# Reciprocal roots of all norms: one power on GpSimd in place of eleven VectorE steps

## The chip, the core and the metric

The kernel runs on one core of a Trainium2 chip. The metric is the time of one execution on the device, in microseconds (us); lower is better. The engines are named as in the profile: PE (TensorE, matrix products and transposes), DVE (VectorE), ACT (ScalarE), POOL (GpSimd) and SP (SyncE, which here issues nearly all DMAs). Each engine works through its own queue strictly in order; an instruction that waits for another engine or for a DMA holds up all that stands behind it on the same engine.

## What is computed

One layer of a hybrid decoder for one sequence of 2048 tokens with 1024 channels, in float32. The root that the change is about stands in `rmsnorm`, which is used for the two layer inputs, for the outputs of the attention and of the state-space model (SSM), and for the final output:

```python
def rmsnorm(x, g):
    y = x32 * lax.rsqrt(jnp.mean(x32 * x32, axis=-1, keepdims=True) + EPS)
    return y * g

h = rmsnorm(x, g_mix) * (1.0 + sc_m) + sh_m          # sc, sh, gt come from silu(c) @ w_ada + b_ada
q, k, v, f_logit, u = jnp.split(h @ w_in, ...)
attn = rmsnorm(forgetting_attention(q, k, v, log_sigmoid(f_logit + b_fgate)), g_attn_out)   # 8 heads of 64
ssm = rmsnorm(s5_ssm(u, ...), g_ssm_out)                                                    # 32 groups of 16
x = x + gt_m * (jnp.concatenate([attn, ssm], axis=-1) @ w_out)
h = rmsnorm(x, g_ffn) * (1.0 + sc_f) + sh_f
gate_pre, val = jnp.split(h @ w_up, 2, axis=-1)                                             # D_FF = 2816
x = x + gt_f * ((silu(causal_dwconv(gate_pre)) * val) @ w_down)
return rmsnorm(x, g_final)
```

## The kernel before

**Work and tiles.** Activations lie with channels on the 128 partitions and tokens along the free axis, in four blocks b = 0 to 3 of 512 tokens. Products are made at nearly full float32 accuracy from a high and a low part of both operands (`hi` and `lo`, three matmuls for each product). So the weights are cast on ACT (`w_hi`, L86 and L121) and their rest is taken on DVE (`w_lo`, L87).

**Order of the stages.** First the inputs of blocks 2, 3, 1 and 0 are normed and projected, with the SSM's tables made beside that; then the SSM; then attention, block by block, mixed with the projections. For each block `mix_t(b)` loads attention and SSM outputs, norms both and transposes the SSM's rows (L1221); `out_proj(b)` multiplies by `w_out` (L1247); `h2_of` norms the result for the feed-forward. Blocks 0 and 1 have their up and down projections (L1273, L1305 to L1307) while attention of blocks 1 to 3 fills the gaps of the other engines. After `out_proj(2)` and `out_proj(3)`, attention is closed; blocks 2 and 3 then go through `up_pair` (L1397) and `down_both` (L1545 to L1547, with L1627) together. At the very end `finish_last` norms and writes block 3 in two halves of 256 tokens (p = 0 and 1).

**A norm's factor.** The squares of all channels are summed into `sq_acc` (L353, L356 and L357), four matmuls with ones (`token_sums`, L365) give the sum of each token as 128x4 numbers in PSUM, `rsqrt_mean` (L182 to L197) makes 1/sqrt(sum/width + eps) of them, four transposes (`over_channels`, L371) spread that over the channels, and ACT copies it to `rt` (L391, or L1713 at the end). There are 21 such roots: 4 for the inputs, 4 each for the SSM and the attention outputs, 4 for the feed-forward inputs, 5 for the outputs (the last block has two).

**The old root.** L185 on DVE makes v = sum/width + eps (`rs_v`). L187 and L188 shift and subtract its bits for a first guess (`rs_i`); three rounds of L193, L194 and L195 refine it (`rs_t`, `rs_y`). All of it works on 128x4 numbers, twice on 128x2.

**The end of attention.** The names for a head pair: L1012, L1013 and L1015 are the scores, ACT L1022 and L1023 the exponentials and their high part, DVE L1024 the low part, DVE L1032 and L1029 the sums, PE L1033 and L1037 the products with the values. When a pair is done: sums to PE (L1061), reciprocal on DVE (L1063), ACT L1065, transposes L1068, scaling on DVE (L1069), a DMA that writes it (L1070). `mix_t` then reads attention (L1208) and SSM rows (L1209), ACT squares the SSM rows (L1211), and after the root DVE scales them (L1217), PE transposes (L1221), ACT applies the gain (L1223) and splits (L400, with DVE L401). `mix_t(3)` puts its rows into the pool `late`.

**What sets the order.** The kernel is written as a tile program; a planner simulates the whole of it with its own costs and writes one fixed order for each engine. `tc.high_priority()` puts a part ahead of others that are ready at the same moment, `tc.issue_after(...)` keeps a part back until an instruction has been placed. So another root can move instructions that have nothing to do with it. `pad` only takes memory, so that the tiles behind it keep their addresses.

Of the kernel before, what the change touches and what calls it, by code (L numbers as in the profile page):

```python
# [12 lines left out]
F32 = mybir.dt.float32  # L13
F32R = mybir.dt.float32r
BF16 = mybir.dt.bfloat16
I32 = mybir.dt.int32
AF = mybir.ActivationFunctionType
ALU = mybir.AluOpType
# [4 lines left out]
P = 128  # L23
# [10 lines left out]
EPS = 1e-6  # L34
NEG = -1e30
WSLOT = 1024
RSQRT_MAGIC = float(0x5F3759DF)
MAGIC = 12582912.0
FFG = (6, 6, 5, 5)
XB = 6  # L40
# [85 lines left out]
def hybrid_layer(ctx, tc, x, c_t, w_ada, b_col, gains, w_flat, bf_row, a_re, a_im, log_dt,  # L126
                 sb_re, sb_im, sc_re, sc_im, dskip, glu, bglu, conv, out):
    nc = tc.nc
    V, A, G, T, Q = nc.vector, nc.scalar, nc.gpsimd, nc.tensor, nc.sync

    const = ctx.enter_context(tc.tile_pool(name="const", bufs=1))
    wpool = ctx.enter_context(tc.tile_pool(name="w", bufs=2))
    small = ctx.enter_context(tc.tile_pool(name="small", bufs=4))
# [3 lines left out]
    def pad(pool, n):  # L137
        if n:
            pool.tile([P, n // 4], F32, name="pad", tag="pad", bufs=1)

    pad(const, 32)
    pad(small, 0)

    @contextmanager
    def behind(ins=None):
# [8 lines left out]
    make_identity(nc, ident)  # L154
    identb = const.tile([P, P], BF16, name="identb")
    V.tensor_copy(identb, ident)
    ones = const.tile([P, 1], F32, name="ones")
    G.memset(ones, 1.0)
    sel = const.tile([P, 2], F32, name="sel")
# [22 lines left out]
    def rsqrt_mean(ss, n, width):  # L182

        v = small.tile([P, 8], F32, name="rs_v")[:, :n]
        V.tensor_scalar(out=v, in0=ss, scalar1=1.0 / width, scalar2=EPS, op0=ALU.mult, op1=ALU.add)  # L185
        i = small.tile([P, 8], I32, name="rs_i", bufs=2)[:, :n]
        V.tensor_scalar(out=i, in0=v.bitcast(I32), scalar1=1, scalar2=None, op0=ALU.logical_shift_right)  # L187
        V.tensor_scalar(out=i, in0=i, scalar1=-1.0, scalar2=RSQRT_MAGIC, op0=ALU.mult, op1=ALU.add)  # L188
        y = i.bitcast(F32)
        for _ in range(3):  # L190
            t = small.tile([P, 8], F32, name="rs_t", bufs=2)[:, :n]
            r = small.tile([P, 8], F32, name="rs_y")[:, :n]
            V.tensor_tensor(out=t, in0=y, in1=y, op=ALU.mult)  # L193
            V.scalar_tensor_tensor(out=t, in0=t, scalar=-0.5, in1=v, op0=ALU.mult, op1=ALU.mult)  # L194
            V.scalar_tensor_tensor(out=r, in0=t, scalar=1.5, in1=y, op0=ALU.add, op1=ALU.mult)  # L195
            y = r
        return y  # L197


    sil = const.tile([P, 8], F32, name="sil")  # L200
# [172 lines left out]
    def norm_sums(acc, ps_fn):  # L373
        ps = ps_fn()
        token_sums(ps, acc, 0, 4)
        return rsqrt_mean(ps[:, 0:4], 4, D)

    def norm_factor(acc, ps_fn, direct=False):

        ps = ps_fn()  # L380
        token_sums(ps, acc, 0, 4)
        r = rsqrt_mean(ps[:, 0:4], 4, D)
        return spread(r, ps_fn, direct)
# [808 lines left out]
    def mix_t(b, tag="row", late_parts=None, ps_fn=None):  # L1192
# [13 lines left out]
        for s in range(4):  # L1206
# [5 lines left out]
            rows.append(t)  # L1212
        res = {}
        rs = rsqrt_mean(ss[:, 0:4], 4, 512)
        for s in range(4):
            f = rows[s][:, 1]
# [570 lines left out]
    for b in range(2):  # L1787
        i = 0
        for g, n in enumerate(FFG):
# [10 lines left out]
            for d in range(8):  # L1800
# [9 lines left out]
                if last and d == OPD:  # L1810
                    with behind():
                        r = norm_sums(sq1 if b == 0 else sqb, op_ps)
# [129 lines left out]
```

## Time and profile before

| | |
|---|---|
| time, median of 3 runs | 2587.67 us (2587.0 to 2597.44) |
| the profiled execution: time, span | 2591.18 us, 2589.5 us |
| PE busy | 2494.1 us, 96% of the span, mean granted clock 0.983 |
| DVE busy | 2048.6 us, 79% |
| ACT busy | 1253.0 us, 48% |
| POOL busy | 151.7 us, 6% |
| moved by DMA | 516.37 MB, mean 199 GB/s |

The profiled execution took 3.5 us more than the median, and its time is 1.7 us more than its span. Busy is the time in which an engine had work, whatever its speed: PE is granted a lower clock at some places, and matmuls there count as busy for longer. In a table of windows a row gives the stretch and its length, then for PE, PEld (weight loads), DVE, ACT and POOL the busy us with the number of instructions, then PE's granted clock (1.00 is full), the share of time that the DMA engines were busy, and GB/s. In a row of a timeline the columns are start, duration, engine, line, operation, what is written and read, shape and count, and in brackets the idle time of this engine before it and what ended that.

### The profile page before, as it was taken

The numbers are of one execution on the slowest core, as the hardware profiler recorded it, in microseconds if no ns is written. First come the engines' busy times: TensorE is split into PE (matmuls) and PEld (weight loads), VectorE is DVE, ScalarE is ACT, GpSimd is POOL, SyncE is SP. The second block draws the span as 40 slices with busy tenths as digits, with TensorE's granted clock in tenths as the row PEclk, the third lists the DMA queues.
The fourth block names the chain that finished last, engine by engine and source line by source line (L and its number), as shares of the span: only waits on it lengthen the run. The fifth ranks groups of instructions, "written<-read, shape, count | busy, mean of one in ns | idle before, by whom it ended". The sixth has DMA issues, their size and how long they took to land.

```text
span 2589.5 us, 35781 instructions
## 1 busy us (share of the span) xinstructions
PE 2494.1 (96%) x12107; PEld 2044.2 (79%) x12107; DVE 2048.6 (79%) x3954; ACT 1253.0 (48%) x2122; POOL 151.7 (6%) x160
## 2 busy tenths in 40 slices
PE   6899999998999999999999999999989999999997
PEld 3788877887788888888878888888768888887876
DVE  7989688976787878877877777776589889886777
ACT  3323255654454545555555655556554555553213
POOL 0001000000000000000000000000002333320000
PEclk8999999999899999999999999999999999999998
DMA  8477987667556655656556555556733443447573
GB/s 313 153 256 223 309 257 210 200 184 244 178 185 219 209 185 184 196 179 211 189 198 226 185 179 186 177 184 219 256 101 130 166 160 134 159 153 286 196 279 119
DMA packets 269608, 516.37 MB, mean 199 GB/s; under 512 B 27985, under 2 KB 114897, under 8 KB 269425
## 3 DMA queue, kind: packets, MB, share of 16 engines
q1 hardware_dynamic: 267600, 508.84, 59.6%
q0 software_dynamic: 1280, 4.20, 0.4%
q8 instruction: 96, 1.57, 0.3%
q10 hardware_dynamic: 544, 1.05, 0.1%
q14 instruction: 88, 0.71, 0.1%
HBM read 374.32 MB, written 139.59 MB: 198 GB/s over the span
## 4 chain that ended last, share of the span: by engine, by line
PE 73%; DMA 10%; DVE 10%; ACT 2%; issue 2%; SPq 2%; POOL 0%; POOLq 0%; ACTq 0%; DVEq 0%
PE ff_ps L1273 18%; PE ff_ps L1247 6%; PE up_x L1397 5%; PE up_z L1397 4%; PE up_y L1397 4%; PE ff_ps L1305 3%; PE ff_ps L1307 3%; PE ff_ps L1306 3%; PE o_ps L1033 2%; PE o_ps L1037 2%; DMA wada<-in_w_ada 2%; PE qs_ps L485 2%; PE acc_x L1627 2%; DMA w_raw<-in_w_flat 2%; PE vq_ps L485 1%
## 5 line engine op out<-in xcount | busy, mean ns | idle before, releaser
L86 ACT CAST w_hi<-w_raw 128x1024 fp32r<-128x1024 f32 (+4 forms) x187 | 173.6, 929 | 273.3 <-DMA w_raw<-in_w_flat 63.4
L1273 PE MATMUL ff_ps<-h_hi,w_hi 128*128 128x512 f32 x704 | 276.7, 394 | 1.0 <-ACT h_hi L403 0.8
L1273 PE MATMUL ff_ps<-h_hi,w_lo 128*128 128x512 f32 x704 | 276.7, 393 | 0.9 <-DMA w_lo<-wlo 0.9
L1273 PE MATMUL ff_ps<-h_lo,w_hi 128*128 128x512 f32 x704 | 276.8, 393 | 0.0
L87 DVE TENSOR_TENSOR w_lo<-w_raw,w_hi 128x1024 fp32r<-128x1024 f32 (+4 forms) x187 | 199.6, 1067 | 54.1 <-ACT w_hi L86 48.9
L1024 DVE TENSOR_TENSOR pl<-pf,ph 128x512 fp32r<-128x512 f32 (+1 forms) x320 | 194.5, 617 | 23.3 <-ACT ph L1023 22.6
L1023 ACT CAST ph<-pf 128x512 fp32r<-128x512 f32 (+1 forms) x320 | 178.0, 568 | 58.6 <-PE o_ps L1033 54.8
L1032 DVE TENSOR_TENSOR acc<-acc,pf 128x512 f32<-128x512 f32 (+2 forms) x264 | 159.2, 604 | 45.1 <-ACT pf L1022 39.5
L1273 PEld LDWEIGHTS ff_ps<-h_hi,w_hi 128*128 128x128 f32 x704 | 132.7, 189 | 29.0 <-ACT h_hi L403 1.5
L1273 PEld LDWEIGHTS ff_ps<-h_hi,w_lo 128*128 128x128 f32 x704 | 132.8, 189 | 28.6 <-DMA w_lo<-wlo 1.3
L1022 ACT ACTIVATE pf<-sc_ps 128x512 f32<-128x512 f32 (+3 forms) x184 | 96.6, 528 | 121.0 <-PE sc_ps L1013 74.7
L1273 PEld LDWEIGHTS ff_ps<-h_lo,w_hi 128*128 128x128 f32 x704 | 132.8, 189 | 27.5 <-issue 0.3
L121 ACT CAST w_hi<-w_raw 128x1024 fp32r<-128x1024 f32 (+2 forms) x100 | 96.7, 967 | 106.2 <-PE ff_ps L1273 50.8
L1306 PE MATMUL ff_ps<-act_lo,w_hi 128*128 128x512 f32 x352 | 138.2, 393 | 0.0
L1307 PE MATMUL ff_ps<-act_hi,w_lo 128*128 128x512 f32 x352 | 138.1, 393 | 0.0
L1305 PE MATMUL ff_ps<-act_hi,w_hi 128*128 128x512 f32 x352 | 137.8, 394 | 0.0
L1033 PE MATMUL o_ps<-ph,vv 128*128 128x512 f32 (+1 forms) x320 | 121.2, 379 | 1.7 <-ACT ph L1023 1.5
L1037 PE MATMUL o_ps<-pl,vv 128*128 128x512 f32 (+2 forms) x312 | 116.6, 376 | 2.1 <-DVE pl L1024 1.9
L1397 PE MATMUL up_x<-hh,w_hi 128*128 128x512 f32 x352 | 110.9, 395 | 3.4 <-ACT hh L400 1.9
L1397 PE MATMUL up_z<-hh,w_hi 128*128 128x512 f32 x308 | 96.6, 395 | 3.1 <-ACT w_hi L86 3.1
L86 ACT CAST w_hi<-s 128x1024 fp32r<-128x1024 f32 (+2 forms) x66 | 62.3, 947 | 72.9 <-DVE s L1598 32.4
L1021 POOL MEMSET pf<- 128x128 f32 x32 | 6.6, 206 | 1401.7 <-DVE pl L1024 1171.9
(673 smaller groups left out, 6928.2 us busy)
## 6 DMA issues: line engine op xcount, KB each, us to landing
w_raw<-in_w_flat SPq DMA_DIRECT2D x193, 512.0 KB
w_lo<-wlo SPq DMA_DIRECT2D x68, 512.0 KB
wlo<-w_lo SPq DMA_DIRECT2D x52, 512.0 KB
kb<-kb SPq DMA_DIRECT2D x80, 256.0 KB
vv<-v SPq DMA_DIRECT2D x80, 256.0 KB
w_raw<-in_w_flat SPq DMA_DIRECT2D x40, 384.0 KB
w_raw<-in_w_flat SPq DMA_DIRECT2D x40, 320.0 KB
wada<-in_w_ada SPq DMA_DIRECT2D x48, 256.0 KB
```

What stands on the lines that cost most here:

```text
L86: nc.scalar.copy(hi[:, :n], raw[:, :n])
L87: nc.vector.tensor_tensor(out=lo[:, :n], in0=raw[:, :n], in1=hi[:, :n].bitcast(F32), op=ALU.subtract)
L1023: A.copy(ph[:, cs], pf[:, cs])
L1024: V.tensor_tensor(out=pl[:, cs], in0=pf[:, cs], in1=ph[:, cs].bitcast(F32), op=ALU.subtract)
L1032: eng.tensor_tensor(out=acc[j][:, cs], in0=acc[j][:, cs], in1=pf[:, cs], op=ALU.add)
L1033: T.matmul(o_ps[:, cs], lhsT=vt[:, i, :], rhs=ph[:, cs], start=first, stop=False)
L1037: T.matmul(o_ps[:, cs], lhsT=vt[:, i, :], rhs=pl[:, cs], start=False, stop=(b > 0 and ch == b - 1 and i == 3))
L1273: T.matmul(ps, lhsT=lt, rhs=rt, start=(n == 0), stop=(n == 23))
L1305: T.matmul(ps, lhsT=a, rhs=ah[:, ts], start=(c == 0), stop=False)
L1306: T.matmul(ps, lhsT=a, rhs=al[:, ts], start=False, stop=False)
L1307: mark[0] = T.matmul(ps, lhsT=bb, rhs=ah[:, ts], start=False, stop=(c == n - 1))
L1397: mark[0] = T.matmul(ps, lhsT=lt, rhs=rt, start=(first and n == 0), stop=(n == 11), skip_group_check=not first)
```

## The change

`rsqrt_mean` keeps L185 on DVE and then raises v to the power -0.5 in one `tensor_tensor` on GpSimd, with a constant tile `mhalf` (128x8, all -0.5) as exponent. The eleven other DVE instructions of each root are gone: 231 in all. DVE has 3725 instructions in its queue in place of 3956, POOL 187 in place of 165 (21 powers and one memset); PE, ACT and SP have as many as before. `mhalf` takes the 32 bytes that a pad held, and the 128 bytes of the tiles `rs_i` and `rs_t` become a pad, so no other tile moves.

```diff
-RSQRT_MAGIC = float(0x5F3759DF)
...
-    pad(const, 32)
-    pad(small, 0)
+    pad(small, 128)
...
+    mhalf = const.tile([P, 8], F32, name="mhalf")
+    G.memset(mhalf, -0.5)
...
     def rsqrt_mean(ss, n, width):
         v = small.tile([P, 8], F32, name="rs_v")[:, :n]
         V.tensor_scalar(out=v, in0=ss, scalar1=1.0 / width, scalar2=EPS, op0=ALU.mult, op1=ALU.add)
-        i = small.tile([P, 8], I32, name="rs_i", bufs=2)[:, :n]
-        V.tensor_scalar(out=i, in0=v.bitcast(I32), scalar1=1, scalar2=None, op0=ALU.logical_shift_right)
-        V.tensor_scalar(out=i, in0=i, scalar1=-1.0, scalar2=RSQRT_MAGIC, op0=ALU.mult, op1=ALU.add)
-        y = i.bitcast(F32)
-        for _ in range(3):
-            t = small.tile([P, 8], F32, name="rs_t", bufs=2)[:, :n]
-            r = small.tile([P, 8], F32, name="rs_y")[:, :n]
-            V.tensor_tensor(out=t, in0=y, in1=y, op=ALU.mult)
-            V.scalar_tensor_tensor(out=t, in0=t, scalar=-0.5, in1=v, op0=ALU.mult, op1=ALU.mult)
-            V.scalar_tensor_tensor(out=r, in0=t, scalar=1.5, in1=y, op0=ALU.add, op1=ALU.mult)
-            y = r
-        return y
+        r = small.tile([P, 8], F32, name="rs_y")[:, :n]
+        G.tensor_tensor(out=r, in0=v, in1=mhalf[:, :n], op=ALU.pow)
+        return r
```

In the changed kernel a line from 37 on has a number one higher than before, from 140 on two higher, and from 186 on nine lower: L1247 is L1238 there, L1070 is L1061. The power is L187. Outside these rows the text uses the numbers of the kernel before. The planner's order differs in many places; three are shown.

**The end of attention, PE.** Before, the last sums of attention (L1061, behind the last two value products L1033 and L1037) are followed at once by matmuls of `out_proj(2)` (L1247 reading `h_hi` and `h_lo`), of which 122 stand between L1061 and the first L1247 that reads `hh`, the first product of `out_proj(3)`:

```order
L1247 MATMUL ff_ps<-h_hi,w_hi 128x512
L1061 MATMUL sc_ps<-sel,sums 128x2
L1033 MATMUL o_ps<-ph,vv 128x512
L1061 MATMUL sc_ps<-sel,sums 128x2
L1037 MATMUL o_ps<-pl,vv 128x512
L1061 MATMUL sc_ps<-sel,sums 128x2 x2
L1247 MATMUL ff_ps<-h_lo,w_hi 128x512
```

Now the last matmul of `out_proj(2)` (the L1238 below) stands ahead of the last 27 attention products, and these, the sums (L1052), the transposes of the pair (L1059), the token sums (L356) and the transposes of the SSM rows (L1212) follow each other with nothing between. Where `out_proj(2)` ends in PE's queue:

```order
L1024 MATMUL o_ps<-ph,vv 128x512
L1238 MATMUL ff_ps<-h_hi,w_lo 128x512
L1028 MATMUL o_ps<-pl,vv 128x512
L1024 MATMUL o_ps<-ph,vv 128x512
L1003 MATMUL sc_ps<-qb,kb 128x512
```

There its last matmul has come to stand among the last value products. Some 20 attention products further on, from the last value product to the first product of `out_proj(3)`:

```order
L1028 MATMUL o_ps<-pl,vv 128x512
L1052 MATMUL sc_ps<-sel,sums 128x2 x4
L1059 MATMUL sc_ps<-ident,sums 128x128 x4
L356 MATMUL qs_ps<-ones,sq_att 128x1 x4
L1212 MATMUL up_y<-ident,row 128x128 x16
L1238 MATMUL ff_ps<-hh,w_hi 128x512 x2
L1238 MATMUL ff_ps<-hh,w_lo 128x512
```

So the 122 matmuls of `out_proj(2)` that stood behind the end of attention now stand ahead of it.

**The same place, SP.** Before, the write of the last pair (L1070) and the row loads (L1208, L1209) stand in the middle of `out_proj(2)`, around the write of its third and fourth result (L1252 into `x_2_2`, `x_2_3`):

```order
L1252 DMA x_2_2_141<-row 128x512
L78 DMA w_raw<-in_w_flat 128x1024
L120 DMA w_lo<-wlo_7539 128x1024
L1070 DMA att_126<-at 128x512
L1252 DMA x_2_3_142<-row 128x512
L78 DMA w_raw<-in_w_flat 128x1024
L1208 DMA row<-att_126 128x512
L1209 DMA row<-ssm_130 128x512
```

Now they stand behind the write of the eighth and last (`x_2_7`):

```order
L1243 DMA x_2_6_147<-row 128x512
L77 DMA w_raw<-in_w_flat 128x1024
L119 DMA w_lo<-wlo_7297 128x1024
L77 DMA w_raw<-in_w_flat 128x1024
L995 DMA vv<-v_120 128x4x128
L1243 DMA x_2_7_148<-row 128x512
L1061 DMA att_128<-at 128x512
L1199 DMA row<-att_128 128x512
L1200 DMA row<-ssm_132 128x512
```

So the attention output and the rows of `mix_t(3)` have moved behind all of `out_proj(2)`.

**The feed-forward norm of block 0, PE.** Before, 26 matmuls of attention stand between the token sums (L365) and the transposes that spread the factor (L371); the first of them are:

```order
L365 MATMUL ff_ps<-ones,sq_acc 128x1 x4
L1037 MATMUL o_ps<-pl,vv 128x512
L1033 MATMUL o_ps<-ph,vv 128x384
L967 MATMUL vq_ps<-ka_7297,qa_3940 128x512
L1037 MATMUL o_ps<-pl,vv 128x384
```

Now one matmul stands there:

```order
L356 MATMUL ff_ps<-ones,sq_acc 128x1 x4
L1003 MATMUL sc_ps<-qb,kb 128x384
L362 MATMUL ff_ps<-ident,rs_y 128x128 x4
L1004 MATMUL sc_ps<-qa_3877,ka_3881 128x512
L1006 LDWEIGHTS identb
L1006 MATMUL sc_ps<-mask_t,identb 128x128
```

The spreading of the factor moved up past attention work, and with it the first matmul of the up projection (L1273), which stands 7 matmuls behind L371 where it stood 13 behind. At the end of POOL's queue the power of the last half (p = 1) stands behind four multiplications of the first half (L1718).

## The prediction

> **What bounds the kernel now.** I read the page first: busy times, then the chain of work that ended last; then the windows of 50 us, to see where PE is not busy or not at full clock; then the timelines at those places.
>
> ```profile
> span 2589.5 us, 35781 instructions
> PE 2494.1 (96%) x12107; PEld 2044.2 (79%) x12107; DVE 2048.6 (79%) x3954; ACT 1253.0 (48%) x2122; POOL 151.7 (6%) x160
> ...
> PE 73%; DMA 10%; DVE 10%; ACT 2%; issue 2%; SPq 2%; POOL 0%; POOLq 0%; ACTq 0%; DVEq 0%
> ```
>
> PE bounds it: it is idle for 2589.5 - 2494.1 = 95 us in all. A change that touches only DVE and POOL can move the time where PE waits, and nowhere else. These are the windows in which it waits and in which roots lie (after the length: busy us of PE, PEld, DVE, ACT, POOL, then PE's clock):
>
> ```profile
> 50.00:100.00 50.00, 43.00 (x282) 40.01 (x281) 48.98 (x192) 22.24 (x53) 0.00 (x0) 0.81 0.55 183
> 100.00:150.00 50.00, 45.34 (x318) 41.02 (x319) 46.13 (x185) 16.27 (x35) 0.00 (x0) 0.97 0.52 154
> 600.00:650.00 50.00, 42.47 (x227) 35.56 (x226) 32.90 (x72) 17.32 (x29) 1.55 (x3) 0.90 0.70 229
> 650.00:700.00 50.00, 46.12 (x183) 35.35 (x182) 36.65 (x77) 22.14 (x37) 0.21 (x1) 0.84 0.57 192
> 1800.00:1850.00 50.00, 47.09 (x222) 37.46 (x221) 27.17 (x73) 24.60 (x40) 0.00 (x0) 1.00 0.78 280
> ```
>
> The reader should see two things: PE loses about 7 us at 600 and 4 us at 650 to idling and about as much again to the clock, and it loses only 2.9 us at 1800, where attention ends.
>
> **What goes and what comes.** One group of the old steps (min, median and max ns), what POOL has to show (busy us and mean ns of one), and for later a DVE step of attention:
>
> ```profile
> L194 DVE SCALAR_TENSOR_TENSOR rs_t<-rs_t,rs_v x63: 110/161/340, 18.8 to 2580.9; 128x4 f32<-128x4 f32 x57, 128x2 f32<-128x2 f32 x6
> ...
> L1024 DVE TENSOR_TENSOR pl<-pf,ph 128x512 fp32r<-128x512 f32 (+1 forms) x320 | 194.5, 617 | 23.3 <-ACT ph L1023 22.6
> ...
> L1384 POOL TENSOR_TENSOR s<-w_raw,v_raw 128x512 f32<-128x512 f32 x18 | 39.0, 2169 | 0.0
> ...
> L1021 POOL MEMSET pf<- 128x128 f32 x32 | 6.6, 206 | 1401.7 <-DVE pl L1024 1171.9 <-DVE acc L1032 147.3 <-DVE rs_v L185 47.1
> L1718 POOL TENSOR_TENSOR yt<-yt,rt 128x256 f32<-128x256 f32 x7 | 4.9, 727 | 270.2 <-DVE rs_t L193 267.8 <-ACT rt L1713 2.4
> L570 POOL TENSOR_SCALAR_AFFINE_SELECT fg<-fg 128x128 f32<-128x128 f32 x1 | 1.5, 1547 | 0.1
> ...
> L572 POOL TENSOR_SCALAR_AFFINE_SELECT fg<-fg 128x128 f32<-128x128 f32 x1 | 0.3, 293 | 0.1
> ```
>
> 231 DVE steps of 0.16 us are 37 us of DVE work. Nearly all lies beside a busy PE and is worth nothing by itself; what counts is the latency of a root where PE waits for it. One power replaces 11 steps. The trace has no power; between a small fill (0.206) and POOL's slowest two-operand step (128x512, 2.17 us, on 128 times as many numbers) I take 0.3 us with both hand-overs, near the small end because 128x4 numbers are few, and keep 0.2 to 2.2.
>
> The Trainium skill ("GPSIMD Engine Reference", section 3.1) has a rule against this change: elementwise work belongs on VectorE, GpSimd being about twice as slow on two operands. As an estimate from that page, twice a 0.16 us step is 0.32 us, but one power stands for eleven steps, so by the rule, too, the root gets shorter.
>
> **Term 1, the last norm.** Rows of DVE, PE, ACT and POOL:
>
> ```profile
> 2571.97 0.15 DVE L185 TENSOR_SCALAR rs_v<-misc_ps 128x2 f32<-128x2 f32 x1
> ...
> 2575.50 0.45 PE L371 MATMUL misc_ps<-ident,rs_y 128*128 128x128 f32 x1 [4.29 <-DVE rs_y L195]
> ...
> 2581.36 0.66 PE L371 MATMUL misc_ps<-ident,rs_y 128*128 128x128 f32 x2 [4.46 <-DVE rs_y L195]
> ...
> 2577.45 2.77 POOL L1718 TENSOR_TENSOR yt<-yt,rt 128x256 f32<-128x256 f32 x4 [267.84 <-DVE rs_t L193]
> 2582.59 2.10 POOL L1718 TENSOR_TENSOR yt<-yt,rt 128x256 f32<-128x256 f32 x3 [2.36 <-ACT rt L1713]
> ```
>
> PE has nothing else left here, so latency is time. From L185 to L371 the first half takes 3.5 us; with a power it is 0.15 + 0.3 + hand-over, say 0.7, and since two more additions (L357) now stand ahead of L185 on DVE, I allow 1.1: a gain of 2.4. The second power is queued on POOL behind four multiplications, 2.77 us. So from the first L371: 1.2 us to POOL's start (as from 2581.36 to 2582.59), 2.8 for these four, 0.3 for the power, 1.2 again, 2.1 for the last three: 7.6, against 9.2 before (2575.50 to 2584.69), 1.6 more. Of the 4.0 I take -3.5, since the output DMAs stand in part behind each other; between 0 (power 2.2 us) and -5.
>
> **Term 2, the feed-forward norm of block 0.**
>
> ```profile
> 679.70 0.15 DVE L185 TENSOR_SCALAR rs_v<-ff_ps 128x4 f32<-128x4 f32 x1
> ...
> 687.42 0.14 DVE L195 SCALAR_TENSOR_TENSOR rs_y<-rs_t,rs_y 128x4 f32<-128x4 f32 x1
> ...
> 690.22 1.05 PE L371 MATMUL ff_ps<-ident,rs_y 128*128 128x128 f32 x4
> ...
> 696.38 1.22 PE L1273 MATMUL ff_ps<-h_hi,w_hi 128*128 128x512 f32 x2 [0.77 <-ACT h_hi L403]
> ...
> 695.00:700.00 5.00, 4.24 (x12) 3.04 (x11) 5.00 (x11) 3.13 (x7) 0.00 (x0) 0.50 0.38 114
> ```
>
> The root takes 7.7 us because its steps queue among attention's on DVE; until L1273 PE has only thin attention work, and its clock falls to 0.50. In the new order L371 comes one matmul behind the sums and L1273 soon after, so PE gets its dense work some 8 to 10 us earlier. The window from 650 holds 3.9 us of idling and, at a clock of 0.84, 7.4 us of lost speed, most of it here; I take near half of the 11, -5, since the eight pairs of `h_hi` and `h_lo` still come one after another; between 0 and -9.
>
> **Term 3, the attention norm of block 0.**
>
> ```profile
> 616.62 0.75 DVE L1128 SCALAR_TENSOR_TENSOR ada_mid<-wada,sil,ada_mid 128x512 f32<-128x512 f32 x1 [2.88 <-DMA wada<-in_w_ada]
> ...
> 619.96 0.80 PE L967 MATMUL qs_ps<-ka,qa 66*128 66x512 f32 x1 [5.14 <-DVE mx L971]
> ...
> 622.19 0.45 PE L371 MATMUL ff_ps<-ident,rs_y 128*128 128x128 f32 x1
> ...
> 623.29 0.63 PE L1247 MATMUL ff_ps<-yt,w_lo 128*128 128x512 f32 x1
> 623.72 0.63 PE L1247 MATMUL ff_ps<-yt,w_hi 128*128 128x512 f32 x1
> ...
> 620.00:625.00 5.00, 4.29 (x10) 2.79 (x11) 3.97 (x8) 0.00 (x0) 0.00 (x0) 0.50 0.97 313
> ```
>
> PE idles 5.1 us since DVE, in order, stands at L1128 waiting for a DMA, with L971 and the root's last steps behind it. In the new DVE order L971 comes ahead of L1128, and the power needs DVE for L185 only. Against that, block 0's attention ends some 75 short matmuls later on PE. The window from 600 holds 7.5 us of idling and 4 us of lost speed; I take half, -6; between 0 and -9.
>
> **Term 4, the start.** DVE is nearly full from 50 to 150 (49.0 and 46.1 of 50), where three roots lie and PE idles 11.7 us. 33 steps of 0.16 are 5.3 us off a full DVE; POOL's table DMAs now wait behind four powers, but they are due only later. I take -4; between 0 and -6.
>
> **Term 5, the end of attention.** Rows of PE, DVE, SP and ACT:
>
> ```profile
> 1826.73 0.39 PE L1247 MATMUL ff_ps<-h_hi,w_hi 128*128 128x512 f32 x1
> 1826.96 0.39 PE L1247 MATMUL ff_ps<-h_lo,w_hi 128*128 128x512 f32 x1
> ...
> 1829.93 0.50 PE L1247 MATMUL ff_ps<-hh,w_hi 128*128 128x512 f32 x1
> ...
> 1804.85 0.69 DVE L1069 TENSOR_TENSOR at<-at,sc_ps 128x512 f32<-128x512 f32 x1 [2.67 <-PE sc_ps L1068]
> ...
> 1807.38 0.99 SPq L1208 DMA_DIRECT2D row<-att  x1
> ...
> 1813.99 0.63 ACT L1211 ACTIVATE h_f<-row 128x512 f32<-128x512 f32 x1 [1.49 <-DMA row<-ssm]
> ...
> 1819.67 0.17 DVE L185 TENSOR_SCALAR rs_v<-ss 128x4 f32<-128x4 f32 x1 [1.50 <-ACT h_f L1211]
> ...
> 1822.59 1.67 DVE L1217 TENSOR_SCALAR row<-row,rs_y 128x512 f32<-128x512 f32 x4
> ```
>
> From L1069 to L185 the pair's write, the row loads and the squares take 14 us, and 10 more go by until the first product of `out_proj(3)`. PE does not notice, for 122 matmuls of `out_proj(2)` (0.227 us each, 28 us) stand beside it. In the new order they are all ahead, and this chain is bare. Step by step, PE's own work taken off: the last eight value steps need two DVE instructions of about 0.62 us each against four matmuls of 0.23 on PE, 2 us of waiting (an estimate: a quarter of a us each); sums, reciprocal, transposes and L1069, some seven dependent steps of 0.2 to 0.7 us, 4; write, loads and squares 14, of which I take 12 since fewer weights load beside them; root 0.5; L1217 1.7; from the first transposes to the first product 3.0 (1826.96 to 1829.93), of which PE works 1.7, so 1.3. That is 21.5, less 0.2 that PE waits in this stretch now, plus 1.6 us for a restart at half clock (after the 5.14 us wait matmuls came every 0.43 us, eight of them; 0.23 is usual), less 2 to 3 of the waits just behind, since weights and ACT run ahead meanwhile. I take +20; between +10 and +26. The shorter root is worth 2.5 us of this and is counted.
>
> The other roots lie beside a full PE: 0; cover is the product running there, and without it each would give back some 2 us.
>
> **The sum.** -3.5 - 5 - 6 - 4 + 20 = +1.5 us on the profiled execution's 2591.18. That execution lies 3.5 us over the median, so against 2587.67 the forecast is 2589 us: no change that a measurement of this kernel can tell, for which I take 0.5% or 13 us (2574.7 to 2600.6).
>
> **Rivals.** *Slower:* the end of attention is dearer, because the eight loads can't start before the write has landed and the SP queue holds them behind the last result of `out_proj(2)`: +26, and the gains at 600 to 700 turn into later waits, because attention, which lags some 100 matmuls there, fills less afterwards: -3 for both. Sum -3.5 - 3 - 4 + 26 = +15.5: 2603 us. It decides from about +25 in term 5 on. For it: the 14 us are measured; against it: the DMA engines are free there. 0.24.
>
> *Faster:* terms 1 to 4 near their far ends, -24, with term 5 at +10, if the loads run in 6 us with nothing beside them: 2574 us. 0.13.
>
> *The power is slow:* at 2.2 us each, some seven that lie bare cost 1.9 more: +13, 2602 us. A first use could cost extra: L570 took 1.55 us where its like take 0.29, which would be 1.3 us, once. 0.08. The Trainium skill ("GPSIMD Engine Reference", section 2.1) gives about 6 us for the first call of freshly loaded code; no run here shows that.
>
> *The change does nothing but reorder:* then all of it is the order of term 5 against 2 and 3, which is within the likeliest.
>
> **Chances and range.** Likeliest, 2580 to 2599: 0.55. Of the slower rival and the slow power most lies above 2600.6: slower 0.27; faster 0.14; the same 0.59. The range from 2575 to 2606 leaves out about 2 in 10.
>
> **What will show it.** PE idle for about 20 us in one stretch around 1815 to 1845, ended by L1221 and the first L1247 reading `hh`; no wait of 5 us before L967 near 615; L1273 starting about 8 us sooner after L365; two waits of 1 and 4 us in place of 4.3 and 4.5 in the tail; a power well under 1 us. I am wrong if PE has work at the end of attention after all, or if the power takes over 1 us.

## The result, and the profile after

The changed kernel takes 2617.56 us (median of 6 runs, 2611.18 to 2618.8) against 2596.22 us for the kernel before in the same comparison (6 runs): the ratio is 1.0083, 95% interval 1.006 to 1.0106, so it is slower by about 21 us. The forecast was 2589 us with a range up to 2606, and no change as the likeliest. In the later comparisons, with more runs, the kernel before lies at 2590 to 2591 us, so 21 us is rather too little than too much: on the two profiled executions the difference is 27.6 us.

The head of the page of the changed kernel and the shares of its chain that ended last:

```profile
span 2616.6 us, 35600 instructions
...
PE 2499.3 (96%) x12107; PEld 2052.2 (78%) x12107; DVE 2023.6 (77%) x3723; ACT 1254.2 (48%) x2122; POOL 175.6 (7%) x182
...
PE 76%; DVE 9%; DMA 9%; issue 2%; ACT 2%; SPq 1%; POOL 0%; POOLq 0%; DVEq 0%; ACTq 0%
```

DVE has 25 us less work, and the span is 27 us longer: PE idles 117 us in place of 95, and its busy time has grown by 5 us at a lower mean clock (0.976, 0.983 before). The windows of 50 us, in the columns of the prediction's table, with the stretch from 300 and the one from 1850 besides:

```profile
50.00:100.00 50.00, 40.38 (x265) 37.64 (x264) 46.32 (x160) 22.89 (x55) 1.48 (x1) 0.84 0.58 190
100.00:150.00 50.00, 50.00 (x370) 47.04 (x370) 44.29 (x165) 18.09 (x43) 2.42 (x2) 0.93 0.64 192
...
300.00:350.00 50.00, 40.40 (x244) 36.75 (x243) 24.52 (x45) 9.88 (x17) 1.00 (x2) 0.86 0.96 307
...
600.00:650.00 50.00, 41.25 (x241) 36.48 (x240) 29.92 (x57) 22.45 (x44) 2.78 (x4) 0.86 0.72 233
650.00:700.00 50.00, 44.26 (x196) 35.08 (x195) 29.05 (x51) 15.52 (x22) 2.06 (x3) 0.94 0.66 219
...
1800.00:1850.00 50.00, 44.21 (x184) 33.03 (x183) 31.91 (x53) 28.51 (x49) 0.21 (x1) 0.90 0.48 164
1850.00:1900.00 50.00, 38.40 (x169) 31.57 (x170) 25.88 (x45) 27.74 (x47) 2.99 (x3) 0.82 0.57 187
```

From 50 to 150 us PE now idles 9.6 us (11.7 before), so a little is won there; from 600 to 700 it idles 14.5 (11.4 before); from 1800 to 1900, 17.4 and part of that at a lower clock. From 300 to 350 it idles 9.6 at 0.86; there it idled 5.7 at 0.97 before (the row stands with the experiments on the start).

**A ledger of the shift.** Windows at fixed times compare different work once one kernel lags. So I add up PE's busy time times its granted clock in windows of 10 us from the start, and ask when each kernel has done the same amount. The table gives how much later (+) than the kernel before each got through a stretch, named by the times of the kernel before: the start (to 410 us), block 0's norms and output products (410 to 709), the stretch behind them with block 1's norms and block 0's last (709 to 1388), and the end of attention (1738 to 1891). The tail is the time from the first L1627 that reads `ring` into `acc_z` to the end of the span, 224.1 us in the kernel before. Each row is one profiled execution. Some rows show how far two executions of one order stand apart: PE's order in `tail_only` is that of before up to the last norm, in `late_powers` up to 1420 us, in `no_start`, `block0_late` and `all_but_six` up to 594 us. These read -0.1 to +4.2 at the start, the first two -0.3 and -4.3 at block 0 and +2.1 and +2.5 from 709 to 1388. So steps below some 5 us are not read from one row. All profiles hold the same 12107 matmul records, but busy time times a window's mean clock is not exactly work: summed over the span it comes to 2463 us before and to 2456 to 2464 us in the others. So a row can add up to some 6 us more than the span's difference. `fewer_loads` leaves out work, and its time is not compared.

| kernel | start | block 0 | 709 to 1388 | end of attention | tail | ratio of the timed runs |
|---|---|---|---|---|---|---|
| changed | +11.3 | +2.7 | +2.0 | +21.2 | -3.4 | 1.0083 [1.006, 1.0106] |
| two_powers | -0.6 | +0.5 | -3.1 | +17.8 | -1.1 | 1.0032 [1.002, 1.0045] |
| two_rounds | -1.5 | -11.1 | +6.5 | +23.7 | -0.2 | 1.0046 [1.0029, 1.0063] |
| hold_out2 | +7.6 | +2.3 | +1.1 | +10.2 | -4.6 | 1.0037 [1.0023, 1.0051] |
| late_powers | +1.1 | -4.3 | +2.5 | +0.9 | -3.6 | 0.9962 [0.9948, 0.9977] |
| start_powers | +5.6 | +3.0 | -0.2 | +2.1 | +0.2 | 1.0037 [1.0023, 1.0051] |
| no_start | +1.7 | -7.2 | 0.0 | +20.3 | -4.2 | 1.0022 [1.0013, 1.0032] |
| block0_late | -0.1 | -6.6 | +5.1 | +1.2 | -3.8 | 0.9974 [0.9965, 0.9983] |
| rounds_then_powers | +3.1 | -12.7 | +6.3 | -0.3 | -3.8 | 0.9954 [0.9941, 0.9967] |
| all_but_six | +4.2 | -6.5 | +8.7 | +1.0 | -4.1 | 1.0005 [0.9994, 1.0017] |
| tail_only | +2.8 | -0.3 | +2.1 | 0.0 | -4.6 | 0.9987 [0.9978, 0.9997] |
| extra_loads | +12.3 | -4.7 | -0.1 | +0.6 | -1.9 | 1.0031 [1.0019, 1.0043] |
| start_pool | +10.7 | -2.1 | +1.4 | +1.9 | 0.0 | 1.0046 [1.0029, 1.0063] |
| before_pool | +7.0 | +7.4 | +0.7 | +0.6 | +0.5 | 1.0029 [1.0019, 1.004] |
| changed_both | +20.7 | -4.1 | +1.5 | +9.8 | -4.3 | 1.0033 [1.002, 1.0047] |
| fewer_loads | +2.7 | -8.9 | -2.5 | +5.9 | -2.9 | - |

So the loss lies in two places, the end of attention, where it was forecast, and the start, where a gain was. Three executions with the changed kernel's order at the start (`changed`, `hold_out2`, `start_powers`) read +11.3, +7.6 and +5.6 there, against -0.6 to +4.2 in the six with the order of before; the last is the fastest of that kernel's five executions. First the end of attention, in the timeline of the changed kernel (PE, then DVE, ACT, SP and POOL):

```profile
1842.62 0.80 PE L1028 MATMUL o_ps<-pl,vv 128*128 128x512 f32 x1
1843.39 1.87 PE L1052 MATMUL sc_ps<-sel,sums 128*128 128x2 f32 x8
1846.21 1.11 PE L1059 MATMUL sc_ps<-ident,sums 128*128 128x128 f32 x4 [0.95 <-ACT sums L1056]
1849.55 1.87 PE L356 MATMUL qs_ps<-ones,sq_att 128*128 128x1 f32 x8 [2.23 <-DVE sq_att L348]
1860.22 1.94 PE L1212 MATMUL up_y<-ident,row 128*128 128x128 f32 x8 [8.80 <-DVE row L1208]
...
1864.41 1.20 PE L1238 MATMUL ff_ps<-hh,w_hi 128*128 128x512 f32 x2
...
1847.36 0.69 DVE L1060 TENSOR_TENSOR at<-at,sc_ps 128x512 f32<-128x512 f32 x1 [1.85 <-PE sc_ps L1059]
1858.23 0.17 DVE L185 TENSOR_SCALAR rs_v<-ss 128x4 f32<-128x4 f32 x1 [6.61 <-ACT h_f L1202]
1858.55 1.98 POOL L187 TENSOR_TENSOR rs_y<-rs_v,mhalf 128x4 f32<-128x4 f32 x2 [50.10 <-DVE rs_v L185]
```

From the last value product to the first product of `out_proj(3)` PE works 9.20 us at half clock in 21.8, where before it was full for 31.7 us. Windows of exactly that stretch, before and after:

```profile
1798.20:1829.90 31.70, 31.70 (x158) 26.45 (x156) 14.49 (x44) 14.25 (x25) 0.00 (x0) 1.00 0.79 282
```

```profile
1842.60:1864.40 21.80, 9.20 (x38) 7.69 (x38) 5.60 (x13) 7.02 (x16) 1.98 (x2) 0.50 0.32 110
```

9.20 us at half clock are 4.6 us of work, so 17.2 us are lost here: 12.6 by idling and 4.6 by the clock. Another 3.4 go in the 42.6 us ahead (PE 39.98 busy at 0.98), where the last value products wait for ACT and DVE.

The power itself, in its group (min, median and max ns), and its first instance:

```profile
L187 POOL TENSOR_TENSOR rs_y<-rs_v,mhalf x21: 698/1009/1855, 17.1 to 2607.7; 128x4 f32<-128x4 f32 x19, 128x2 f32<-128x2 f32 x2
```

```profile
17.10 1.47 POOL L187 TENSOR_TENSOR rs_y<-rs_v,mhalf 128x4 f32<-128x4 f32 x1 [13.54 <-DVE rs_v L185]
```

It takes 1.01 us in the median, three times the 0.3 that I took and half of the upper end. The 0.32 us estimated from the Trainium skill ("GPSIMD Engine Reference", section 3.1) is a third of that; the operation measured in that section is an addition, so the page has no price for a power. The Trainium skill ("GPSIMD Engine Reference", section 2.1) has the first call of freshly loaded code cost about 6 us more. The first power here starts 0.09 us after its input is written (L185 ends at 17.01) and takes 1.47 us, so no cost of that size shows.

The tail, with the two halves' powers and multiplications:

```profile
2602.78 0.15 DVE L185 TENSOR_SCALAR rs_v<-misc_ps 128x2 f32<-128x2 f32 x1
2603.01 0.94 POOL L187 TENSOR_TENSOR rs_y<-rs_v,mhalf 128x2 f32<-128x2 f32 x1 [15.30 <-DVE rs_v L185]
...
2604.01 0.43 PE L362 MATMUL misc_ps<-ident,rs_y 128*128 128x128 f32 x2 [1.33 <-POOL rs_y L187]
2604.99 2.77 POOL L1709 TENSOR_TENSOR yt<-yt,rt 128x256 f32<-128x256 f32 x4 [1.04 <-ACT rt L1704]
...
2608.47 0.69 PE L362 MATMUL misc_ps<-ident,rs_y 128*128 128x128 f32 x2 [3.69 <-POOL rs_y L187]
2609.72 2.09 POOL L1709 TENSOR_TENSOR yt<-yt,rt 128x256 f32<-128x256 f32 x3 [1.30 <-ACT rt L1704]
```

From L185 to the first transposes 1.23 us (3.53 before), from there to the last multiplication's end 7.80 (9.19 before): 3.7 us gained in these rows.

Block 0's two norms in the changed kernel, PE's rows:

```profile
607.59 0.50 PE L1004 MATMUL sc_ps<-qa,ka 67*128 67x512 f32 x1 [3.14 <-DMA qa<-rrow]
630.46 0.51 PE L958 MATMUL qs_ps<-ka,qa 66*128 66x512 f32 x1 [1.47 <-DVE mx L962]
...
692.54 1.05 PE L356 MATMUL ff_ps<-ones,sq_acc 128*128 128x1 f32 x8
695.01 1.11 PE L362 MATMUL ff_ps<-ident,rs_y 128*128 128x128 f32 x4 [1.02 <-POOL rs_y L187]
698.49 1.22 PE L1264 MATMUL ff_ps<-h_hi,w_hi 128*128 128x512 f32 x2
```

The wait of 5.14 us before the reduced scores (L967 there, L958 here) is down to 1.47, and from the token sums to the first up product 5.95 us go by, where from L185 alone it was 16.7 us before.

### The profile page after: what moved, and what is told of

The parts are those of the page before. It is cut to its first block, busy times and chain, and to the rows that moved or that the text cites. A ratio compares the mean times of both kernels' runs of the same rounds, so it can differ in the third digit from the quotient of the medians.

```text
span 2616.6 us, 35600 instructions
## 1 busy us (share of the span) xinstructions
PE 2499.3 (96%) x12107; PEld 2052.2 (78%) x12107; DVE 2023.6 (77%) x3723; ACT 1254.2 (48%) x2122; POOL 175.6 (7%) x182
## 4 chain that ended last, share of the span: by engine, by line
PE 76%; DVE 9%; DMA 9%; issue 2%; ACT 2%; SPq 1%; POOL 0%; POOLq 0%; DVEq 0%; ACTq 0%
PE ff_ps L1264 19%; PE ff_ps L1238 6%; PE up_x L1388 6%; PE up_z L1388 4%; PE up_y L1388 4%; PE ff_ps L1296 3%; PE ff_ps L1297 3%; PE ff_ps L1298 3%; PE o_ps L1024 2%; PE o_ps L1028 2%; DMA w_raw<-in_w_flat 2%; PE acc_x L1618 2%; PE vq_ps L476 1%; DMA wada<-in_w_ada 1%; DVE w_lo L86 1%
```

## The experiments

The 21 roots are numbered in the order of the code: 0 to 3 the inputs, 4 and 5 the SSM and attention outputs of block 0, 6 block 0's feed-forward norm, 7 and 8 the outputs of block 1, 9 block 1's feed-forward norm, 10 the last norm of block 0, 11 to 20 all later ones (19 and 20 the two halves of the last). What a kernel's order says of the end of attention is one number: the matmuls of `out_proj(2)` that stand on PE behind the last head pair's transposes (99 before, none in the changed kernel), called its cover. Where only some roots are powers, the edit is

```diff
+POWERS = (9, 10)
...
     def rsqrt_mean(ss, n, width):
+        if next(count) in POWERS:
...
+            G.tensor_tensor(out=r, in0=v, in1=mhalf[:, :n], op=ALU.pow)
+            return r
```

**What uncovers the end of attention.** `two_powers`: `POWERS = (9, 10)`, two roots that lie 500 us and more ahead of that place; cover 7.

> The kernel before with a power for two of the 21 roots only: the feed-forward norm of block 1 and the output norm of block 0. Both lie in the middle of the run, beside a full PE. In this kernel's fixed order 7 matmuls of out_proj(2) stand behind the transposes of the last head pair, against 99 in the kernel before and 0 in the changed one. Theory A (the order): the bare end of attention costs +15 to +22 us against the kernel before, and nothing else changes. Theory B (the power itself is slow, 1.0 us on average in the changed kernel, and costs where PE waits): two powers beside a full PE cost 0, at most 2 us.

2599.11 us, +8 us. Two powers are enough to uncover the stretch, +17.8 in the ledger. The whole time rose by less than the +15 to +22 expected; some 4 us of the difference are read in other rows (-3.1 and -1.1), the rest is within what the ledger can miss. From the last value product to `out_proj(3)`:

```profile
1814.00:1841.00 27.00, 12.16 (x61) 10.04 (x60) 10.49 (x38) 10.24 (x19) 0.00 (x0) 0.68 0.54 185
```

`two_rounds`: no power and nothing on GpSimd; every root with two rounds of refinement in place of three, so less exact by one; cover 0.

```diff
-        for _ in range(3):
+        for _ in range(2):
```

> No power at all: the kernel before with two refining rounds in place of three on VectorE, all 21 roots (the root is a little less accurate). In its order 0 matmuls stand behind the last pair's transposes, as in the changed kernel; the first part of the program keeps an order near that of before. Theory A (the order): +12 to +22 us, although DVE has 63 instructions less and GpSimd nothing new. Theory B (the power is slow): 0 to -5 us.

2605.64 us, +12 us. The end of attention loses as much (+23.7) without any power. So the loss needs neither GpSimd nor the power's time. With these other roots the planner writes `out_proj(2)` ahead of the last value products, and that is what the two kernels have in common with the changed one. Not every set of shorter roots does it (`late_powers`, below, keeps a cover of 95), and how the planner's simulation gets from the one to the other was not followed. The same kernel gains 11 us at block 0.

`hold_out2`: the changed kernel, with the products of `out_proj(2)` of row blocks 4 to 7 kept back until the last pair's transposes; cover 96.

```diff
-                T.transpose(rp[:, s * P : (s + 1) * P], rx[:, s * P : (s + 1) * P], ident)
+                pair[0] = T.transpose(rp[:, s * P : (s + 1) * P], rx[:, s * P : (s + 1) * P], ident)
...
-                    mark[0] = T.matmul(ps, lhsT=lt, rhs=rt, start=(i == 0), stop=(i == 23))
+                    with tc.issue_after(pair[0].ins) if b == 2 and d >= 4 else nullcontext():
+                        mark[0] = T.matmul(ps, lhsT=lt, rhs=rt, start=(i == 0), stop=(i == 23))
```

> The changed kernel, with all 21 powers, in which the second half of out_proj(2) is kept back in the order until the transposes of the last head pair have been placed: 96 matmuls stand behind them in place of 0; all that comes earlier is in the same order as in the changed kernel. Theory A (the order): -13 to -20 us against the changed kernel, so 0 to +8 us against the kernel before, the rest being the start and block 0. Theory B (the power is slow): +18 to +22 us against the kernel before, no better than the changed kernel.

2601.79 us; against the changed kernel's ratio that is some 12 us less, just short of the 13 to 20 expected. In the stretch PE is busy again, but its clock is lower and the value products ahead now wait uncovered (27.19 us busy in the 30 us before it, 30.00 in the kernel `start_powers`), so half of the loss stays (+10.2 of +21.2):

```profile
1817.80:1851.30 33.50, 30.55 (x134) 25.27 (x134) 12.34 (x23) 14.48 (x27) 1.98 (x2) 0.83 0.58 189
```

**What the late roots are worth.** `late_powers`: `POWERS` from 11 to 20; cover 95.

> The kernel before with a power for the last ten roots only (attention and SSM norms of blocks 2 and 3, and all that comes after), whose order keeps 95 matmuls behind the last pair's transposes. Theory A (the order): no bare end of attention, so only the gain of the tail is left: -3 to -5 us against the kernel before. Theory B (the power is slow): ten powers of 1 us, four or five of them bare: 0 to +5 us.

2582.85 us, 8 us faster than the kernel before and more than the 3 to 5 expected, with PE full in that stretch (below). The tail gives 3.6 us of it. Between 1891 and 2360 us it and the seven other kernels with powers at roots 12 to 18 read -1.9 to -2.9 (`fewer_loads` set aside), the seven without -0.1 to -1.4: some 2 us more. The rest is not located; the -4.3 at block 0 lies ahead of its first power.

```profile
1799.10:1829.80 30.70, 30.70 (x152) 25.66 (x152) 12.43 (x23) 14.71 (x25) 1.99 (x2) 1.00 0.81 291
```

`tail_only`: `POWERS = (19, 20)`, the tail alone.

> Powers at the two roots of the last block alone; no instruction ahead of the last norm is moved on any engine but for buffer numbers. By the forecast's term 1: -3.5 us (0 to -5). With a power of 1.0 us in place of the 0.3 assumed, twice, -2 us.

2587.32 us, -3.4 (by the interval of its ratio -0.8 to -5.7); the tail is 4.6 us shorter in its profile, where kernels without powers there read +0.5 to -1.9. Term 1 stands, though the -2 us that a power of 1 us would give lies in the interval as well.

**The start.** `start_powers`: `POWERS = (0, 1, 2, 3)`; cover 90. `no_start`: all but these; cover 0.

> Powers at the first four roots alone (the norms of the inputs, at the start); all others as before, so 90 matmuls of out_proj(2) stay behind the last head pair's transposes and the end of attention is covered. Theory C (a shorter root at the start makes the planner write another order of projections and table work there, which is worse on the chip): the start, up to the equal work of 350 us, loses 8 to 12 us, and the whole is +8 to +12 us against the kernel before. Theory D (the changed kernel's loss at the start is the latency of a power and a hand-over to GpSimd, at most some 1.1 us in each of four places): 0 to +4 us. By the forecast's term 4 it would be -4 us.

> Powers at all roots but the first four; these keep their old steps, and the order of the start is that of before. No matmul of out_proj(2) is left behind the last head pair's transposes, as in the changed kernel. Theory C: the start loses nothing, the end of attention loses its +20 us, and the whole is +10 to +16 us against the kernel before, some 8 to 12 us below the changed kernel. Theory D: as the changed kernel less at most 4 us, about +17 to +21.

2601.14 us (+9.8) and 2595.73 us (+4.4). Four short roots at the start cost 10 us with the end of attention intact. Without them the changed kernel would be 16 us faster (ratio 1.0022 against 1.0083), more than the +10 to +16 expected allowed for, since block 0 then gains too (-7.2 in place of +2.7). Term 4 has the wrong sign. And it is not four powers' latency: when the last of them is done, at 140.63 us in the changed kernel, PE has not lost anything yet (it is 2.7 us ahead at the equal work of 144 us, 3.2 in `start_powers`). Where PE stands: one row of the kernel before, two of the changed kernel, then `start_powers`, there with the ACT row that PE waits for and SP's rows:

```profile
315.36 0.36 PE L452 MATMUL qs_ps<-w_hi,h_hi 128*128 128x256 f32 x1 [1.50 <-DVE vst L513]
...
289.09 0.33 PE L803 MATMUL prep_ps<-ident,tb_e_re 128*128 128x128 f32 x1 [3.09 <-ACT tb_wb L804]
...
341.75 0.58 PE L443 MATMUL qs_ps<-w_hi,h_hi 128*128 128x256 f32 x1 [4.77 <-DVE vst L504]
...
335.35 0.58 PE L460 MATMUL qs_ps<-w_hi,h_hi 128*128 128x256 f32 x1 [5.86 <-DVE vst L521]
...
334.47 0.37 ACT L520 CAST vst<-qs_ps 128x256 fp32r<-128x256 f32 x1 [7.78 <-DMA v<-vst]
...
315.26 1.31 SPq L936 DMA_DIRECT2D vin<-u_d  x2
...
325.36 1.78 SPq L936 DMA_DIRECT2D vin<-u_d  x2
...
330.23 1.01 SPq L522 DMA_DIRECT2D v<-vst  x2
```

So PE waits 1.50 us for `vst` there in the kernel before, and 4.77, 5.86 and 7.22 us in the three profiles with the changed order (`hold_out2` the last). These three have also a wait for `tb_wb` near 285 us, of 3.09, 2.42 and 2.94, where PE is full in the kernel before. That is where PE stands; for why its operands come late two explanations were tried. By the first (C2 in the expectations) the bytes count: 69.98 MB had been moved by 300 us in the changed kernel and 74.17 before, and the DMA engines are 0.96 busy from 300 to 350 in both. `extra_loads`: the kernel before, with six transfers more behind three of the loads of L1123. `fewer_loads`: the changed kernel with loads of that line left out. It keeps the one for k = 0 in each of the two halves, so 14 of 16 are gone, not 15 as the expectation says.

```diff
-                Q.dma_start(wt, w_ada[sec, k, :, hf * TB : (hf + 1) * TB])
+                ld = Q.dma_start(wt, w_ada[sec, k, :, hf * TB : (hf + 1) * TB])
+                if hf == 0 and k < 3:
+                    for r in range(2):
+                        with tc.issue_after(ld.ins):
+                            Q.dma_start(spare[2 * k + r], w_ada[sec, 2 * k + r])
```

```diff
-                Q.dma_start(wt, w_ada[sec, k, :, hf * TB : (hf + 1) * TB])
+                if k == 0:
+                    keep = wt
+                    Q.dma_start(wt, w_ada[sec, k, :, hf * TB : (hf + 1) * TB])
+                wt = keep
```

> The kernel before with six additional transfers of 512 KB each (3.1 MB, from the array w_ada to an unused buffer in DRAM, read by nothing), two behind each of the first three wada loads of ada_mid (L1123), near 290 to 297 us. Theory C2 (the start ends later in the changed kernel because w_ada's loads are placed later: by 300 us 69.98 MB have been moved there and 74.17 MB in the kernel before, and from 300 to 350 us the DMA engines are 0.95 to 0.96 busy at about 290 GB/s, so each MB that is late costs 3 to 3.5 us): with 3.1 MB more the equal work of 350 us comes +7 to +11 us later. Rival (the number of bytes does not count there; what costs is the order of PE, DVE and ACT): 0 to +2 us there.

> The changed kernel with 15 of the 16 wada loads of ada_mid left out (the first one is used in place of all, so this part of the conditioning is computed from wrong weights); ten of the 16 lie between 300 and 360 us there. PE's order is the same up to about 600 us. Theory C2: some 2.3 MB less in the stretch in which the DMA engines are full, so the equal work of 350 us comes 5 to 8 us sooner than in the changed kernel (+4 to +7 against the kernel before in place of +12). Rival (order of PE, DVE and ACT): at most 2 us sooner. The end of attention has another order there (44 matmuls of out_proj(2) behind the last pair's transposes), so the whole time is not compared.

With the added loads the start is 12.3 us later and the time 7 us longer (2597.69). But the planner wrote another order of PE, DVE, ACT and SP from about 300 us on there, so it is not shown that the bytes themselves cost it. And the loads left out (2581.18 us, not compared as a whole) gave little at this place. The start reads +2.7 in place of +11.3, of which 6.6 were there already at the equal work of 300 us, ahead of the first load left out: two executions of one order differ by as much. From 300 to 350 us it loses 5.9 us, where the three profiles with the changed order lose 7.6, 5.1 and 6.8. The bytes are not shown to be the cause.

By the second (C3), SP's queue counts: from the first SP row above to the write of `v`, the 12 loads of the SSM's first two pairs (`vin`, `tab`, `ft`, `ttg`, `glt`) and two more of `vin` stand ahead of it. `start_pool` has the 12 issued by GpSimd, as in the edit for `tab`, `before_pool` does that to the kernel before, and `changed_both` to the changed kernel together with `hold_out2`'s edit.

```diff
-            Q.dma_start(tab, tab_d[p // 4][p % 4, :, 0:768])
+            (G if p < 2 else Q).dma_start(tab, tab_d[p // 4][p % 4, :, 0:768])
...
```

> As start_powers (powers at the first four roots alone), but the 12 loads of the SSM's first two pairs (vin, tab, ft, ttg, glt) are issued by GpSimd and not by SP. Theory C3 (with short roots the SSM's tables come later, so that these loads stand in SP's queue right ahead of the writes of kb and v, and ACT and PE wait for those): the wait of 5.9 us before L460 for vst goes or falls below 2 us, and 4 to 8 us of the 10 come back: +2 to +6 us against the kernel before. Rival C4 (the SSM's tables and loads are late by themselves, whichever queue issues them): +8 to +12 us, as start_powers.

> The kernel before with the same 12 loads issued by GpSimd; no power. A control for start_pool: in the kernel before the loads stand at 302 to 312 us, ahead of the last projections' writes, and PE waits 1.5 us for vst there. C3: 0 to -3 us against the kernel before. If the move is worth as much here as in start_pool, C3 does not explain what the powers cost.

> The changed kernel (powers at all 21 roots) with both remedies: the 12 loads from GpSimd's queue, and the matmuls of out_proj(2) of the last four of eight row blocks held back until the last head pair's transposes, as in hold_out2. C3 and term 5 together: hold_out2's +10 us less 4 to 8 at the start and less what follows from it near 610 us: 0 to +6 us against the kernel before. C4: as hold_out2, +8 to +12.

2602.11, 2599.42 and 2600.51 us (ratios 1.0046, 1.0029 and 1.0033 [1.002, 1.0047]): nothing came back, and moving the loads costs 8 us even without a power. The wait for `vst` did get shorter, 3.32 us in `start_pool` (less than 2 was expected) and 2.45 in `changed_both`, but one of 4.18 for `w_hi` and one of 5.22 for `mx` came in its place. So this explanation, by which 4 to 8 us would come back, falls. The windows from 300 to 350 us of the kernel before, `start_powers`, `extra_loads` and `before_pool`:

```profile
300.00:350.00 50.00, 44.29 (x282) 39.32 (x281) 24.51 (x54) 16.81 (x32) 0.79 (x3) 0.97 0.96 287
```

```profile
300.00:350.00 50.00, 39.91 (x258) 36.94 (x257) 24.78 (x48) 11.81 (x22) 1.21 (x3) 0.86 0.95 299
```

```profile
300.00:350.00 50.00, 35.76 (x217) 32.38 (x216) 16.80 (x32) 9.07 (x15) 1.00 (x2) 0.86 0.93 282
```

```profile
300.00:350.00 50.00, 42.90 (x278) 39.18 (x277) 21.25 (x46) 14.58 (x27) 8.97 (x15) 0.93 0.86 268
```

PE does 44.29 x 0.97 = 43.0 us of work there before, and 34.3, 30.8 and 39.9 in the others; in the changed kernel 34.7, 8.2 us less, 3.9 of them by idling and 4.3 by the lower clock. What is shown is that three different edits that alter the order between 290 and 340 us each lost 7 to 10 us. Which feature of the order it is stays open.

**Gains without the two losses.** `block0_late`: powers at 4 to 6 and 11 to 20; cover 99. `all_but_six`: powers at all but 0 to 3, 9 and 10; cover 99. `rounds_then_powers`: two rounds at 0 to 6, three at 7 to 11, powers at 12 to 20; cover 90.

```diff
+ROOTS = "222222233333pppppppppp"
...
+        how = ROOTS[next(count)]
...
-        for _ in range(3):
+        for _ in range(int(how)):
```

> Powers at the three roots of block 0 (its SSM, attention and feed-forward norms) and at the ten last roots; old steps at the start and at the four roots between. The end of attention keeps the order of before (99 matmuls of out_proj(2) behind the last pair's transposes). If the forecast's terms 2 and 3 are right where nothing else is moved, -11 us come at 600 to 710 beside the tail and the other late roots (about -10): -13 to -20 us against the kernel before. If block 0 goes as in the changed kernel (about +2 there), -8 us, within 3.

> Powers at all roots but six: the four of the start, block 1's feed-forward norm and block 0's last norm keep their old steps. The start has the order of before, and 99 matmuls of out_proj(2) stay behind the last head pair's transposes. If the losses of the changed kernel come from the two places (the start, and the end of attention) and its gains from the roots themselves: block 0 -5 to -7, tail and other late roots -4 to -8, in all -8 to -14 us against the kernel before. If every set of powers moves something of its own, -3 to -8, as with the three roots of block 0 and the ten last.

> No power before block 1's last norm: two rounds instead of three at the first seven roots (less exact by one refinement), three rounds at the next five, powers at the last nine; 90 matmuls of out_proj(2) stay behind the last pair's transposes. If block 0 gains what it gained with two rounds everywhere (-11 us up to the equal work of 709 us) and the late roots what late powers alone gave (about -8 to -10), -15 to -20 us against the kernel before. If block 0's gain depends on the order around the other roots, -5 to -10 us.

2585.03, 2591.89 and 2579.41 us. All three read less at block 0 (-6.6, -6.5, -12.7) and keep the end of attention, but each gives 5 to 9 us back between 709 and 1388 us, as `two_rounds` does. So the expected sums were missed, by `all_but_six` altogether, and in the time the powers at block 0 add nothing to those at 11 to 20 (`block0_late` 0.9974, `late_powers` 0.9962). Why the gain goes is open: `no_start`, with powers at block 1 too, gives nothing back there, but `two_rounds`, whose roots are shorter at block 1 too, does. `rounds_then_powers` is the fastest kernel here (ratio 0.9954), and not told apart from `late_powers` (0.9962), which refines the early roots fully. Its page and its window of block 0's attention norm, where PE was busy 42.47 us at 0.90 before:

```profile
span 2578.5 us, 35705 instructions
...
PE 2488.9 (97%) x12107; PEld 2042.2 (79%) x12107; DVE 2034.2 (79%) x3834; ACT 1253.5 (49%) x2122; POOL 161.1 (6%) x170
```

```profile
600.00:650.00 50.00, 47.94 (x279) 41.14 (x279) 36.57 (x72) 21.20 (x33) 1.56 (x3) 1.00 0.84 277
```

## Why the prediction was wrong

On the profiled executions the forecast was +1.5 us, the result +27.6 (2618.8 against 2591.18). Two places carry the miss: the start, +11.3 in the ledger in place of -4, and block 0, +2.7 in place of -11.

- **Term 5, the end of attention: right.** +20 forecast, +21.2 in the ledger. Of its steps, write, loads and squares took 10.2 us from the end of L1060 to L185 (12 taken), and from the first L1212 to the first product 4.2 (3.0 taken, read from a matmul of `out_proj(2)` at 1826.96; the first L1221 stands at 1827.19). The split was less good than the sum: idling took 15 us and the lower clock 5, for which I had 1.6, and that these differences cancel is luck. `two_powers` and `two_rounds` show the mechanism without the other changes, and `hold_out2`, which gives back the cover, halves the loss.
- **Term 1, the tail: right.** -3.5 forecast, 2.9 to 4.6 us shorter in every profile with powers there, and -3.4 us timed alone. The power's 0.94 and 0.70 us in place of 0.3 cost little: 1.23 us to the first transposes against the 1.1 reckoned, and 7.8 us from there to the end against 7.6.
- **Term 2, block 0's feed-forward norm: the path right, the gain not shown.** -5 forecast. The norm's way from the sums to the up product is shorter by more than 10 us, as said. But from 650 to 709 us the ledger reads only -1.6 in the changed kernel and -0.3 to -2.5 in the five kernels of the next point, where three profiles with the order of before read 0 to -4.0 (`two_powers`, `tail_only`, `late_powers`). So the half of 11 us that I took was probably too much.
- **Term 3, block 0's attention norm: right where the start is left alone, wrong here.** -6 forecast. From 613 to 630 us, where the wait for `mx` stood, the ledger reads -5.1 to -6.6 in `no_start`, `block0_late`, `all_but_six`, `two_rounds` and `rounds_then_powers`, against +0.8 to +1.3 in the three with the order of before. In the changed kernel it is -1.8, and +6.2 ahead of it, from 561 to 613: new waits came (3.14 us for the DMA `qa<-rrow`), and the output products begin at 636.54, 14 us later than before. This was named under the rival of later waits, but at -3 for both norms together, not as a loss. It goes with the start: `start_powers` alone reads +9.6 from 561 to 613, with old roots at block 0, and `no_start` +0.5. How the one leads to the other was not followed.
- **Term 4, the start: the step that failed.** -4 forecast, +11.3 in the profile and +10 us for these four roots alone. I took 33 DVE steps off a full DVE and costed the new order at nothing but four powers on POOL's queue. PE does gain a little up to 150 us (2.7 at the equal work of 144 us), but the order from 280 to 340, where PE in the kernel before had 5 us of waits, was read for none of the engines. There the waits for `tb_wb` (3.09 us), `qk_lo` (3.52) and `vst` (4.77) and the lower clock took more than was won. That the order does it is shown by `start_powers` and `no_start`; which feature of it stays open.
- **The power's price** was mis-sized, 0.3 us against 1.01, and it did not decide: `two_rounds` has no power and loses 12 us.

Of what was to show it: PE did stand in one stretch ended by L1212 and the first `hh` (12.6 us idle of 21.8, not 20), the wait near 615 fell to 1.47 us, the two waits of the tail are 1.33 and 3.69 us; "a power well under 1 us" did not hold. "The change does nothing but reorder" came nearest to what happened, and I put it within the likeliest case, since I had read only one of the places as a loss.

## What to carry to other kernels

Where a planner writes the whole order, a shorter step is a new order everywhere: compare the two orders along the whole span before costing, and above all where the bounding engine has little slack, not only where the edited step lies. Take a change apart by instance, for here the same edit is worth -8 us at ten late places, +10 us at four early ones, and +8 us at two that lie 500 us ahead of what they disturb; the version to keep is the one whose covers stay (`late_powers`). A gain read halfway is not yet a gain in the time: three kernels read 6 to 13 us less at block 0 and had given 5 to 9 of it back 700 us later.

## What the runs showed that I had not expected

A power on GpSimd takes 1.01 us in the median of the 21, six times a DVE step on as many numbers (0.16). The longest, over 128x4 numbers, took 1.86, the two over 128x2 took 0.94 and 0.70. Executions of one order differ by 4 to 7 us in how late they stand at 300 to 410 us, which is as much as the terms argued over. And six more transfers (3.1 MB) that nothing reads, in a stretch in which the DMA engines are 0.96 busy, came with a start 12 us later and a time 7 us longer; how much of that is the transfers and how much the order that the planner wrote around them is not separated.
